# Casting and splitting a weight unit in one piece of 2048 columns instead of two

## The chip, the cores and the metric

The kernel runs on one core of a Trainium2 chip. The core has a matrix engine (TensorE, PE in the profile), a vector engine (VectorE, DVE), a scalar engine (ScalarE, ACT), GpSimd (POOL) and SyncE (SP), which here issues the loads. Each engine works through its own queue in order; semaphores hold an instruction back until what it reads is there. The metric is the time of one execution in microseconds (us), the median of several runs.

## The reference

Two layers over 256 tokens of width 1024, in f32. Each layer projects the normed tokens with one wide matrix, runs two branches (a chunked gated linear attention in both directions, and a grouped-query attention with rotary positions), merges them behind sigmoid gates, and adds an FFN of hidden width 2816 and a gated embedding:

```python
u = rms_norm(h, g_mix_pre)
(gq, gk, gv, gg, ra_f, ra_b, aq, ak, av, gate_a, gate_b) = jnp.split(u @ w_in, offsets, axis=-1)
...
branch_a = (o_gla * jax.nn.silu(gg)) @ w_o_gla
...
branch_b = gqa_attention(q, k, v) @ w_o_attn
mixed = jax.nn.sigmoid(gate_a) * branch_a + jax.nn.sigmoid(gate_b) * branch_b
h = h + rms_norm(mixed @ w_out, g_mix_post)
gate, up = jnp.split(rms_norm(h, g_ffn_pre) @ w_ffn_in, 2, axis=-1)
h = h + rms_norm((jax.nn.silu(gate) * up) @ w_ffn_out, g_ffn_post)
e = p_i @ w_ple_proj
h = h + rms_norm(jax.nn.sigmoid(h @ w_ple_gate) * e, g_ple_post)
```

All weights together are about 160 MB and are read once; the tokens stay on the chip.

## The kernel before

Every matrix product is done as three products of parts in fp32r, a narrower form of f32: each operand x is split into hi = x cast to fp32r and lo = x - hi, and `mm3` (line 96) adds hi x hi, hi x lo and lo x hi in PSUM. So each weight must be cast and split on the chip before TensorE can use it. ACT makes the cast (line 110), DVE the subtraction (line 106), both in `split`.

The weights come in units of 1 MB: 128 partitions by 2048 columns (2112 for the units of the first projection), which is 512 rows of a matrix by 512 of its columns, laid out as four steps of 128 rows, or 256 rows by 1024. The list `plan` holds all 170 units in the order in which they are used. `Stream` carries them:

- `start` issues the loads on SP into raw buffers (pool `rawp`, two of them; in the FFN some units are loaded into borrowed buffers instead, the `lent` and `big` tiles).
- `put` (line 263) takes a pair of buffers wh and wl (pool `wp`, four pairs), puts them on the list `ready`, and gives the cuts in which the unit is to be split: two halves of 1024 columns. The callers `made` and `fill` run `split` on each cut: a cast to wh on ACT and a subtraction to wl on DVE.
- `take` (line 315) hands the oldest unit of `ready` to the matmuls; `done` (line 319) says that a unit is used up, and `fill` then makes the next one, until `held` units (ready or in use) reach `depth`, which is 4, and 3 in the stretch of the linear attention, where a pair of buffers holds that branch's values.

`ready` is a list at the time when the program is written out: it tells how many units stand in program order ahead of the matmuls that are still to come, not how many are finished on the chip at some moment. `open` becomes true after the first units of the start-up, which are ordered by hand.

The order of the instructions in each engine's queue isn't the program's own: a scheduler lays it out when the program is built, by priority (the program's order, moved forward by `tc.high_priority` for norms, transposed activations and some evictions) and by when it expects an instruction's inputs. `tc.issue_after` fixes an order by hand in some places. On the chip each queue runs in the order laid out.

Other parts that the steps below touch: `by_half` takes four units at once and uses them for the first and then the second 128 tokens, as do the first two FFN blocks; `seven` computes two FFN blocks with seven products instead of eight, for which `step` adds raw units on DVE (lines 287 to 298, 2048 columns each) and line 582 combines products; `transpose_in` (line 402) and `turn` transpose activations on TensorE and split them; `pre_norm` and `post_norm_add` compute the norms (squares on ACT line 440, root on POOL, scaling on DVE lines 460 and 500). In names of tiles the number is the layer and the word the stage: rq and kv are the first projections, gqk, v and gg those of the linear attention, then gate, merge, wout, ffnin, ffnout, emb and ple.

Of the kernel before, what the change touches and what calls it, by code (L numbers as in the profile page):

```python
# [48 lines left out]
def trunk_kernel(ctx: ExitStack, tc: tile.TileContext, a: dict, out: bass.AP):  # L49
# [21 lines left out]
    def nm(s):  # L71
        uid[0] += 1
        return f"{s}_{part[0]}_{uid[0]}"
# [134 lines left out]
    class Stream:  # L208
# [51 lines left out]
                    between()  # L260
                x.n = sum(math.prod(dst.shape[1:]) for dst, _ in moves)

        def put(self, x, parts=2):

            wh = wp.tile([P, UNIT], F32R, tag="wh", name=nm("wh"))
            wl = wp.tile([P, UNIT], F32R, tag="wl", name=nm("wl"))
            self.ready.append((wh, wl))
            self.held += 1
            cuts = [slice(j * x.n // parts, (j + 1) * x.n // parts) for j in range(parts)]
            return [(wh[:, c], wl[:, c], x.raw[:, c]) for c in cuts]  # L270

# [1164 lines left out]
```

## Time and profile before

| what | value |
|---|---|
| time, three runs | 934.88, 935.49, 937.68 us; median 935.49 |
| profiled execution, span from first to last instruction | 937.3 us |
| granted TensorE clock over the span | 0.999 |
| PE / weight loads / DVE / ACT busy | 922.6 / 783.9 / 732.4 / 561.6 us |
| casts of units on ACT | 340, two for each of 170 units |
| subtractions of units on DVE | 340 |
| data read from memory | 167.41 MB, 180 GB/s over the span |

The profiled execution's own time is told only as its span, 937.3 us; that is 1.8 us above the median of the runs and within their spread. In the rows of the profile, "x2" is the number of instructions in the row, the two numbers at the head of a timeline row are its start and length in us, and what stands in square brackets is the engine's idle time before the row and what ended it. In rows of groups, busy time and the mean in ns follow the first bar, idle time the second. A matmul's end is modelled, so PE's pace is read from starts.

### The profile page before, as it was taken

The page shows a single profiled execution, that of the slowest core. Times are in us where ns is not written, and L with a number is a line of the kernel's source. Part 1 is how long each engine was busy: PE and PEld are TensorE (multiplying, and loading weights), DVE is VectorE, ACT ScalarE, POOL GpSimd, SP SyncE. Part 2 cuts the span into 40 slices and gives each one's busy share as a digit, 9 for nine tenths or more (in the row PEclk, how much of TensorE's full clock was granted, in tenths as well). Part 3 has the DMA queues.
Part 4 walks back from the last instruction along what each step waited for, and adds up shares of the span by engine and source line. Part 5 has one row for each costly group of instructions (what it writes and reads, how often), then busy time and mean ns, then how long its engine had stood idle before and what let it go on. Part 6 is the DMA issues. An engine that isn't in the chain of part 4 may idle for free.

```text
span 937.3 us, 12331 instructions
## 1 busy us (share of the span) xinstructions
PE 922.6 (98%) x4697; PEld 783.9 (84%) x4697; DVE 732.4 (78%) x933; ACT 561.6 (60%) x928; POOL 80.8 (9%) x150
## 2 busy tenths in 40 slices
PE   8999999999999999999999999999999999999996
PEld 6998888888878878888899988888888788888786
DVE  4798978456569899999689799674666798989874
ACT  4669676443457565567666686754435666656563
POOL 3400214000000000000022001200001000000000
PEclk9999999999999999999999999999999999999999
DMA  6464455665275565547455525365553937463551
GB/s 229 168 223 137 136 191 191 191 213 180 91 249 169 203 233 190 203 143 249 167 175 181 192 78 180 116 244 181 200 190 103 310 114 268 154 266 112 180 180 45
DMA packets 88089, 169.26 MB, mean 181 GB/s; under 512 B 3351, under 2 KB 26391, under 8 KB 88030
## 3 DMA queue, kind: packets, MB, share of 16 engines
q1 hardware_dynamic: 88030, 168.47, 52.8%
q8 instruction: 37, 0.61, 0.3%
q14 instruction: 22, 0.18, 0.1%
HBM read 167.41 MB, written 1.05 MB: 180 GB/s over the span
## 4 chain that ended last, share of the span: by engine, by line
PE 79%; DVE 9%; DMA 4%; ACT 3%; issue 3%; POOL 1%; SPq 0%; POOLq 0%; ACTq 0%; DVEq 0%
PE acc_1ffnin L94 9%; PE acc_0ffnin L94 8%; PE acc_0gate L94 5%; PE acc_1gate L94 5%; PE acc_1merge L94 5%; PE acc_0merge L94 5%; PE acc_0ffnin L543 4%; PE acc_1ffnin L543 4%; PE acc_1gqk L94 2%; PE acc_0rq L94 2%; PE acc_0gqk L94 2%; PE acc_1ple L94 2%; PE acc_0gg L94 2%; PE acc_1gg L94 2%; PE acc_1v L94 2%
## 5 line engine op out<-in xcount | busy, mean ns | idle before, releaser
L94 PE MATMUL acc_1ffnin<-wh_1ffnin,big_1ffnin 128*128 128x512 f32 x176 | 56.9, 393 | 0.0
L94 PE MATMUL acc_0ffnin<-wh_0ffnin,big_0ffnin 128*128 128x512 f32 x176 | 56.8, 392 | 0.0
L110 ACT CAST wh_1ffnin<-raw_1ffnin 128x1024 fp32r<-128x1024 f32 x38 | 38.1, 1050 | 23.1 <-PE acc_1ffnin L94 7.7
L110 ACT CAST wh_0ffnin<-raw_0ffnin 128x1024 fp32r<-128x1024 f32 x38 | 37.9, 1049 | 22.0 <-PE acc_0ffnin L94 7.9
L106 DVE TENSOR_TENSOR wl_1ffnin<-raw_1ffnin,wh_1ffnin 128x1024 fp32r<-128x1024 f32 x38 | 44.8, 1219 | 5.6 <-ACT wh_1ffnin L110 5.4
L106 DVE TENSOR_TENSOR wl_0ffnin<-raw_0ffnin,wh_0ffnin 128x1024 fp32r<-128x1024 f32 x38 | 44.7, 1219 | 3.9 <-ACT wh_0ffnin L110 3.9
L94 PEld LDWEIGHTS acc_1ffnin<-wh_1ffnin,big_1ffnin 128*128 128x128 f32 x176 | 33.0, 188 | 7.1 <-ACT big_1ffnin L110 0.4
L94 PEld LDWEIGHTS acc_0ffnin<-wh_0ffnin,big_0ffnin 128*128 128x128 f32 x176 | 33.0, 188 | 6.7
L106 DVE TENSOR_TENSOR wl_0ffnin<-lent_0ffnin,wh_0ffnin 128x1024 fp32r<-128x1024 f32 x30 | 35.5, 1218 | 1.9 <-ACT wh_0ffnin L110 1.7
L106 DVE TENSOR_TENSOR wl_1ffnin<-lent_1ffnin,wh_1ffnin 128x1024 fp32r<-128x1024 f32 x30 | 35.4, 1218 | 2.0 <-ACT wh_1ffnin L110 2.0
L110 ACT CAST wh_1ffnin<-lent_1ffnin 128x1024 fp32r<-128x1024 f32 x30 | 30.2, 1049 | 9.0 <-PE acc_1ffnin L94 3.0
L110 ACT CAST wh_0ffnin<-lent_0ffnin 128x1024 fp32r<-128x1024 f32 x30 | 30.2, 1049 | 8.4 <-PE acc_0ffnin L94 3.7
L94 PE MATMUL acc_0ffnin<-wl_0ffnin,big_0ffnin 128*128 128x512 f32 x88 | 34.3, 389 | 0.0
L94 PE MATMUL acc_1ffnin<-wl_1ffnin,big_1ffnin 128*128 128x512 f32 x88 | 34.3, 389 | 0.0
L94 PE MATMUL acc_1ffnin<-wh_1ffnin,big_1wout 128*128 128x512 f32 x96 | 31.2, 394 | 0.0
L94 PE MATMUL acc_0ffnin<-wh_0ffnin,big_0wout 128*128 128x512 f32 x96 | 31.2, 394 | 0.0
L543 PE MATMUL acc_0ffnin<-wh_0ffnin,mid_0ffnin 128*128 128x512 f32 x96 | 31.0, 390 | 0.0
L543 PE MATMUL acc_1ffnin<-wh_1ffnin,mid_1ffnin 128*128 128x512 f32 x96 | 31.0, 390 | 0.0
L106 DVE TENSOR_TENSOR wl_0gate<-raw_0gate,wh_0gate 128x1024 fp32r<-128x1024 f32 x14 | 16.5, 1221 | 17.8 <-ACT wh_0gate L110 17.8
L106 DVE TENSOR_TENSOR wl_1gate<-raw_1gate,wh_1gate 128x1024 fp32r<-128x1024 f32 x14 | 16.5, 1221 | 17.8 <-ACT wh_1gate L110 17.8
L94 PE MATMUL acc_0rq<-wh_start,big_start 128*128 128x384 f32 (+1 forms) x96 | 25.4, 349 | 1.4 <-ACT big_start L120 1.4
L94 PE MATMUL acc_0gate<-wh_0gate,big_start 128*128 128x512 f32 x80 | 24.8, 389 | 0.0
(647 smaller groups left out, 2931.3 us busy)
## 6 DMA issues: line engine op xcount, KB each, us to landing
raw_0ffnin<-in_w_ffn_out_dram SPq DMA_DIRECT2D x11, 1024.0 KB, 5.3
raw_1ffnin<-in_w_ffn_out_dram SPq DMA_DIRECT2D x11, 1024.0 KB, 5.9
lent_0ffnin<-in_w_ffn_in_dram SPq DMA_DIRECT2D x6, 1024.0 KB, 8.7
lent_1ffnin<-in_w_ffn_in_dram SPq DMA_DIRECT2D x6, 1024.0 KB, 7.8
raw_0rq<-in_w_in_dram SPq DMA_DIRECT2D x4, 1024.0 KB, 5.2
raw_0v<-in_w_in_dram SPq DMA_DIRECT2D x4, 1024.0 KB, 5.0
raw_0gg<-in_w_in_dram SPq DMA_DIRECT2D x4, 1024.0 KB, 5.1
raw_0gate<-in_w_o_gla_dram SPq DMA_DIRECT2D x4, 1024.0 KB, 5.2
```

The costliest lines, as they stand in the source:

```text
L94: return nc.tensor.matmul(o, lhsT, rhs, start=start, stop=stop)
L106: nc.vector.tensor_tensor(out=out, in0=in0, in1=in1, op=ALU.subtract)
L110: nc.scalar.copy(hi, src)
L543: nc.tensor.matmul(o, x, y, start=first and k + n == 0, stop=k == 3 and n == 2, skip_group_check=not first)
```

## The change

`put` takes its number of pieces from the state of the stream: one piece where the stream is open and the list `ready` holds another unit besides the new one, two where it doesn't. The one piece is one cast of 2048 columns on ACT and one subtraction of 2048 columns on DVE, which waits for the whole cast. Loads, buffers and matmuls are as before.

```diff
-        def put(self, x, parts=2):
+        def put(self, x, parts=None):
 
             wh = wp.tile([P, UNIT], F32R, tag="wh", name=nm("wh"))
             wl = wp.tile([P, UNIT], F32R, tag="wl", name=nm("wl"))
             self.ready.append((wh, wl))
             self.held += 1
+            parts = parts or (1 if self.open and len(self.ready) > 1 else 2)
             cuts = [slice(j * x.n // parts, (j + 1) * x.n // parts) for j in range(parts)]
             return [(wh[:, c], wl[:, c], x.raw[:, c]) for c in cuts]
```

## The prediction, made before the changed kernel was run

> **What bounds the kernel now.** I read the page first: the busy shares, then the chain that ended last.
>
> ```profile
> span 937.3 us, 12331 instructions
> ...
> PE 922.6 (98%) x4697; PEld 783.9 (84%) x4697; DVE 732.4 (78%) x933; ACT 561.6 (60%) x928; POOL 80.8 (9%) x150
> ...
> PE 79%; DVE 9%; DMA 4%; ACT 3%; issue 3%; POOL 1%; SPq 0%; POOLq 0%; ACTq 0%; DVEq 0%
> ```
>
> TensorE (PE) is busy 922.6 of 937.3 us, so it is the bound, and all of its idle time together is 14.7 us. That includes the start, where the first load is waited for, and the tail, where the last norm and the store run after the last matmul. An edit that touches no matmul can win only a part of these 14.7 us. What it can lose has no such limit: each time PE must wait longer for a weight unit, the end moves by that much. The chain says who is last when PE does wait: in 9% of the span VectorE (DVE), in 4% a transfer, in 3% ScalarE (ACT). So next I asked how full DVE is, stage by stage, by windows (columns: PE, PEld, DVE, ACT, POOL busy, granted clock, DMA share, GB/s), here for the FFN stage of each layer.
>
> ```profile
> 283.00:437.00 154.00, 153.32 (x697) 126.25 (x696) 144.90 (x141) 95.81 (x120) 1.82 (x3) 1.00 0.56 195
> ...
> 742.00:896.00 154.00, 152.36 (x690) 124.85 (x690) 142.65 (x138) 94.28 (x118) 0.86 (x2) 1.00 0.55 194
> ```
>
> In the FFN, DVE is busy 144.90 of 154 us, 94%, and PE still only idles 0.7 us. DVE is nearly a second bound there, but the queue of finished units hides it. The clock granted is 1.00 in both, so it plays no part.
>
> **The price of one piece.** The groups by line and shape, and one stretch of the chain that gives PE's pace:
>
> ```profile
> L110 ACT CAST wh_0gate<-raw_0gate 128x1024 fp32r<-128x1024 f32 x14 | 14.0, 1052 | 14.0 <-PE acc_0gate L94 13.9
> ...
> L106 DVE TENSOR_TENSOR wl_0gate<-raw_0gate,wh_0gate 128x1024 fp32r<-128x1024 f32 x14 | 16.5, 1221 | 17.8 <-ACT wh_0gate L110 17.8
> ...
> L287 DVE TENSOR_TENSOR lent_0ffnin<-lent_0ffnin,lent_0ffnin 128x2048 f32<-128x2048 f32 x3 | 6.9, 2285 | 0.0
> ...
> 418.63 5.44 PE acc_0ffnin L543 x24
> ```
>
> A cast of 1024 columns takes 1.05 us, a subtraction 1.22 us. A DVE tensor_tensor of 2048 columns in f32 exists already (line 287): 2.285 us. Two halves back to back take 2.35 or 2.36 us (rows below), so one piece saves 0.07 us of DVE. For the cast no 2048 row exists. It lies between 1.85 us (if only 0.80 us were added to 1.05) and 2.00 us, which is what two halves take back to back in the rows below. I take 1.90 us, because merging on DVE saved a little less than 0.1 us too. PE's pace is 5.44/24 = 0.23 us a matmul.
>
> [...]
>
> How many units: each layer's plan has 4 rank units, 22 of the projection, 8 merge, 4 w_out, 42 FFN, 1 embedding and 4 gate units, 85, so 170. Three are made before the stream is open, and five with nothing else ready (the first unit after w_out, after the four units that the FFN takes at once, and after the first layer's last gate stage). The other 162 become one piece: 162 casts and 162 subtractions fewer, about 16 us less ACT and 11 us less DVE. In the gate rows the casts' idle time is ended by PE (13.9 of 14.0): there a unit is made as soon as a buffer comes free, three units ahead of its use. In these stages I cost the edit at nothing, and the lead of several us is the cover. No DMA is added or moved on SP's queue. A raw buffer comes free 0.07 us earlier where the halves ran back to back, and about 0.8 us later where DVE had stood waiting for the cast.
>
> That is the catch. With halves, DVE starts 1.05 us after the cast does, and after about 2.3 us PE can use the first half (two of the unit's four contraction steps). With one piece, hi is there after 1.90 us and lo after 1.90 + 0.04 + 2.285 = 4.23 us, 1.9 us later for the first use. Being "ready" is counted when the program is written out, not by time: a unit whose load lands late is number three or four of the list and is just as late. So I looked for each place where PE takes a unit within 2 us of its completion, or waits for a DVE result queued behind one.
>
> **B and C, FFN entry, layers 0 and 1** (timelines of ACT, DVE and PE):
>
> ```profile
> 264.10 2.00 ACT L110 CAST wh_0wout<-raw_0wout 128x1024 fp32r<-128x1024 f32 x2 [1.94 <-DMA raw_0wout<-in_w_ffn_in_dram]
> 265.19 2.36 DVE L106 TENSOR_TENSOR wl_0wout<-raw_0wout,wh_0wout 128x1024 fp32r<-128x1024 f32 x2 [0.48 <-ACT wh_0wout L110]
> 266.47 0.50 PE L94 MATMUL acc_0ffnin<-wl_0wout,big_0wout 128*128 128x512 f32 x1 [0.23 <-DVE wl_0wout L106]
> 269.36 1.38 PE L402 MATMUL aux_0wout<-ident,mid_0wout 128*128 128x128 f32 x8
> 269.89 2.35 DVE L106 TENSOR_TENSOR wl_0wout<-raw_0wout,wh_0wout 128x1024 fp32r<-128x1024 f32 x2
> 271.16 0.50 PE L94 MATMUL acc_0ffnin<-wl_0wout,big_0wout 128*128 128x512 f32 x1 [0.18 <-DVE wl_0wout L106]
> ...
> 721.98 2.01 ACT L110 CAST wh_1wout<-raw_1wout 128x1024 fp32r<-128x1024 f32 x2 [1.06 <-DMA raw_1wout<-in_w_ffn_in_dram]
> 723.39 2.35 DVE L106 TENSOR_TENSOR wl_1wout<-raw_1wout,wh_1wout 128x1024 fp32r<-128x1024 f32 x2
> 724.84 0.39 PE L94 MATMUL acc_1ffnin<-wl_1wout,big_1wout 128*128 128x512 f32 x1
> 727.92 2.35 DVE L106 TENSOR_TENSOR wl_1wout<-raw_1wout,wh_1wout 128x1024 fp32r<-128x1024 f32 x2
> 729.19 0.50 PE L94 MATMUL acc_1ffnin<-wl_1wout,big_1wout 128*128 128x512 f32 x1 [0.18 <-DVE wl_1wout L106]
> ```
>
> The cast waits for its transfer, and PE waits for the first half. In one piece: cast 264.10 to 266.00, subtraction 266.04 to 268.33, first lo use 268.37 instead of 266.47, 1.90 us late. PE then has eleven matmuls (2.50), eight transposes (0.87 at the 0.11 us they take start to start) and one matmul (0.23), 3.60 us, and would reach the next unit's lo at 271.97. It is there at 269.89 + 2.285 + 0.04 = 272.21 instead of 271.16. The short waits that PE has in between now vanish in this, so the net loss is 1.05 us. Layer 1 the same way: cast to 723.88, lo at 726.24 instead of 724.84 (1.40 late); the next unit is reached at 729.84 and ready at 730.24 against 729.19: 1.05 us.
>
> **A, first keys unit of layer 0.** DVE is full of rotary work:
>
> ```profile
> 45.01 1.21 DVE L106 TENSOR_TENSOR wl_0rq<-raw_start,wh_0rq 128x1024 fp32r<-128x1024 f32 x1
> ...
> 46.28 0.50 PE L94 MATMUL acc_0kv<-wl_0rq,big_start 128*128 128x512 f32 x1 [0.15 <-DVE wl_0rq L106]
> ...
> 46.61 1.21 DVE L106 TENSOR_TENSOR wl_0rq<-raw_start,wh_0rq 128x1024 fp32r<-128x1024 f32 x1
> ```
>
> One piece from 45.01 ends at 47.30, so PE goes on at 47.35 instead of 46.28: 1.07 us.
>
> **D, end of the FFN, layer 0 and layer 1, and F, the second pair's start:**
>
> ```profile
> 427.78 2.00 ACT L110 CAST wh_0ffnin<-raw_0ffnin 128x1024 fp32r<-128x1024 f32 x2 [0.75 <-DMA raw_0ffnin<-in_w_ffn_out_dram]
> 429.11 2.35 DVE L106 TENSOR_TENSOR wl_0ffnin<-raw_0ffnin,wh_0ffnin 128x1024 fp32r<-128x1024 f32 x2
> 430.50 0.40 PE L94 MATMUL acc_0ffnin<-wl_0ffnin,big_0ffnin 128*128 128x512 f32 x1
> ...
> 877.30 2.00 ACT L110 CAST wh_1ffnin<-raw_1ffnin 128x1024 fp32r<-128x1024 f32 x2 [4.51 <-DMA raw_1ffnin<-in_w_ffn_out_dram]
> 878.39 2.36 DVE L106 TENSOR_TENSOR wl_1ffnin<-raw_1ffnin,wh_1ffnin 128x1024 fp32r<-128x1024 f32 x2 [1.73 <-ACT wh_1ffnin L110]
> 884.14 0.68 DVE L103 TENSOR_TENSOR t_1ffnin<-mid_1ffnin,t_1ffnin 128x512 f32<-128x512 f32 x1
> 884.88 0.66 PE L402 MATMUL aux_1ffnin<-ident,t_1ffnin 128*128 128x128 f32 x4 [1.48 <-DVE t_1ffnin L103]
> 886.46 2.00 ACT L110 CAST wh_1ffnin<-raw_1ffnin 128x1024 fp32r<-128x1024 f32 x2
> 890.15 0.40 PE L94 MATMUL acc_1ffnin<-wl_1ffnin,big_1ffnin 128*128 128x512 f32 x1
> ...
> 327.00 2.00 ACT L110 CAST wh_0ffnin<-raw_0ffnin 128x1024 fp32r<-128x1024 f32 x2 [1.21 <-DMA raw_0ffnin<-in_w_ffn_in_dram]
> 330.36 0.68 DVE L582 TENSOR_TENSOR mid_0ffnin<-acc_0ffnin,mid_0ffnin 128x512 f32<-128x512 f32 x1
> 331.19 0.47 PE L543 MATMUL acc_0ffnin<-wh_0ffnin,big_0wout 128*128 128x512 f32 x1 [0.55 <-DVE mid_0ffnin L582]
> ```
>
> Layer 0 at 430: cast to 429.68, lo at 432.04 against 430.50: 1.54 us. Layer 1: DVE starts the unit at 879.24 instead of 878.39 and is done 0.78 us later; one more unit in between gives 0.07 back, so the product that PE's transposes await moves from 884.14 to 884.86, 0.72 us. The cast at 886.46, behind these transposes, moves to 887.18, lo is there at 891.44 against 890.15: 1.29 us in all. F: cast to 328.90, DVE to 331.23; the combination behind it (line 582), which frees PE's accumulator, starts at 331.15 instead of 330.36: 0.79 us.
>
> **E, hand-over to layer 1.** PE waits for a unit's second half, then for the norm:
>
> ```profile
> 481.97 0.41 PE L94 MATMUL acc_1rq<-wl_0ple,big_0ple 128*128 128x288 f32 x1 [0.39 <-DVE wl_0ple L106]
> ...
> 483.57 0.66 PE L402 MATMUL aux_0ple<-ident,mid_0ple 128*128 128x128 f32 x4 [0.53 <-DVE mid_0ple L460]
> ```
>
> The unit would come later, but PE waits for the norm at 483.57 anyway. A whole unit on DVE ahead of the norm's steps can hold it about 1.2 us (half a unit), and a raw buffer freed sooner can start the last load 1.2 us sooner. Between -1.2 and +1.2 I take 0.
>
> **Sum.** 1.07 + 1.05 + 1.05 + 1.54 + 1.29 + 0.79 = 6.79 us. For the shorter DVE queue I take off 0.4 us: in each FFN one wait behind three merged units, 3 x 0.07 twice. Net +6.4 us on a span of 937.3. The profiled span lies 1.8 us above the median of the runs, 935.49, so the forecast is 935.5 + 6.4 = 941.9 us. If no wait in between is absorbed (B 1.90, C 1.40, E 1.2) the loss is about 10 us. If the order of DVE's work is written out anew so that half of the places vanish, it is 3 us. I cannot see that order: the engines' queues are laid out by priority and expected readiness, and fewer, longer instructions can change it.
>
> **Rivals.** (1) Faster. DVE is at 94% in the FFN; its relief there is 38 units x 0.07 = 2.7 us a layer, and the waits at 331.19 and 884.88 (0.55 and 1.48 us) end on DVE. If the queue ahead of such a wait holds several merged units and no late cast, PE gets it all: about 3.2 us from both, with the short waits, 932.3 us. It decides if the unit ahead is not held by its transfer. Against it: at both places DVE's queue begins with a late load. [...] (2) No change: the late first halves are absorbed by other waits or taken out by a new order. What remains is 0 to 2.5 us, about 936.5 us. For it: at B a loss of 1.90 shrinks to 1.05 within 5 us, and E to nothing. (3) Worse: each late unit also frees its raw buffer 0.8 us late, and with two such buffers the next-but-one load is late too. Where loads set the casts (all FFN ends), three or four links add 5 us: 947 us or more. Against it, most units have leads of over 2 us.
>
> **Chances.** Forecast 0.52, rival 1 0.15, rival 2 0.25, rival 3 0.08. About 0.3%, 2.8 us, is what a measurement can tell from no change. Slower by more than that: 0.60, same 0.25, faster 0.15. The range of the forecast alone is 938.5 to 946 us; with the rivals down to a tenth below and a little above, 933 to 947 us.
>
> **What would show it.** The casts and subtractions of units: 178 of each instead of 340, at 1.90 and 2.29 us. PE's idle time up by some 6 us, as waits on a lo tile at the FFN entry (lo use 1.9 us after now) and near 430 and 890, and on line 582 near 331. DVE's busy time about 721 us, ACT's about 546. PE's matmul busy time per stage unchanged. I am wrong if the FFN entry shows no longer wait, if PE's idle time falls below 14 us, or if the cast of 2048 columns takes well under 1.85 us.

## The result, and the profile after

The changed kernel takes 960.48 us (median of four runs, 955.97 to 961.37); the kernel before took 936.22 us beside it. The ratio is 1.0236, 95% interval 1.0218 to 1.0254: 24 us slower, where the prediction said 6.4. The profiled execution has a span of 958.5 us, 21.2 more than before. First the page, with the groups of the new pieces in the FFN:

```profile
span 958.5 us, 12013 instructions
...
PE 930.7 (97%) x4697; PEld 787.6 (82%) x4697; DVE 722.1 (75%) x771; ACT 547.6 (57%) x766; POOL 89.3 (9%) x150
...
PE 74%; DVE 9%; DMA 7%; ACT 4%; issue 3%; POOL 2%; SPq 0%; POOLq 0%; ACTq 0%; DVEq 0%
...
L110 ACT CAST wh_0ffnin<-raw_0ffnin 128x2048 fp32r<-128x2048 f32 x19 | 36.1, 1913 | 32.5 <-PE acc_0ffnin L94 10.2
...
L106 DVE TENSOR_TENSOR wl_0ffnin<-raw_0ffnin,wh_0ffnin 128x2048 fp32r<-128x2048 f32 x19 | 43.3, 2290 | 12.2 <-ACT wh_0ffnin L110 12.1
```

The pieces cost what they should: 1.91 us a cast, 2.29 a subtraction. 162 instructions fewer stand on each of the two engines, DVE is busy 10.3 us less and ACT 14.0 less. All of it came off engines whose total is not the bound, and PE stands idle 27.8 us instead of 14.7. PE's waits, longest first (total us, times, longest):

```profile
PE aux_1ffnin L1259 <- DVE t_1ffnin L103: 3.9, 1, 3.9
PE acc_0ffnin L94 <- DVE wl_0wout L106: 2.4, 2, 1.8
PE aux_0ffnin L1259 <- DVE t_0ffnin L103: 2.0, 1, 2.0
PE acc_0kv L94 <- DVE wl_0rq L106: 2.0, 1, 2.0
PE aux_0ple L403 <- DVE mid_0ple L461: 1.9, 2, 1.2
PE acc_1ffnin L94 <- DVE wl_1wout L106: 1.6, 2, 1.1
...
PE aux_1at L94 <- DVE big_1kv L106: 1.3, 1, 1.3
PE aux_1at L94 <- ACT big_1kv L110: 0.8, 1, 0.8
PE aux_1at L94 <- DVE mid_1at L106: 0.7, 1, 0.7
```

Rows on wl are waits for a unit: A (wl_0rq), B (wl_0wout) and C (wl_1wout) of the prediction. Rows on t, mid and big are waits for activations, which only stand in the same queues as the units. They are as large, and the prediction has none of them but E (mid_0ple). I call them G (349 us, t_0ffnin), I (819 us, t_1ffnin) and H (531 us, the transposed keys). The third part is PE's clock (windows; the granted clock is the third column from the right):

```profile
48.00:54.00 6.00, 6.00 (x21) 4.74 (x20) 4.69 (x8) 1.75 (x6) 1.04 (x3) 0.72 0.91 312
271.00:275.00 4.00, 3.84 (x20) 3.01 (x20) 3.28 (x3) 3.45 (x5) 0.60 (x2) 1.00 0.73 218
...
353.00:357.00 4.00, 4.00 (x14) 3.18 (x14) 2.07 (x3) 0.79 (x3) 0.00 (x0) 0.61 0.53 127
...
533.64:537.05 3.41, 2.89 (x13) 2.89 (x14) 1.51 (x4) 0.00 (x0) 0.00 (x0) 0.50 0.90 291
...
819.60:823.60 4.00, 0.12 (x1) 0.00 (x0) 4.00 (x5) 1.90 (x1) 0.00 (x0) 1.00 0.01 5
823.60:827.20 3.60, 3.58 (x11) 2.80 (x12) 3.19 (x3) 0.59 (x1) 0.00 (x0) 0.53 0.02 3
```

Behind A, G and I the granted clock of these windows is 0.72, 0.61 and 0.53, and the 512-column matmuls there start 0.43 us apart instead of 0.23. Behind H the window is laid on the slow stretch itself: 0.50 for 3.41 us. The other three slow stretches are as long. Behind the shorter wait B (1.8 us) the clock is 1.00 in the window from 271 us. Worked out from PE's starts over the whole trace, gaps of over 0.25 us beyond the usual distance add some 15 us, and matmuls at a slow pace some 6. Together that is the 21.2 us of the span.

### The profile page after: what moved, and what is told of

It is laid out like the page before. It is cut to its first block, busy times and chain, and to the rows that moved or that the text cites. A ratio compares the mean times of both kernels' runs of the same rounds, so it can differ in the third digit from the quotient of the medians.

```text
span 958.5 us, 12013 instructions
## 1 busy us (share of the span) xinstructions
PE 930.7 (97%) x4697; PEld 787.6 (82%) x4697; DVE 722.1 (75%) x771; ACT 547.6 (57%) x766; POOL 89.3 (9%) x150
## 3 DMA queue, kind: packets, MB, share of 16 engines
HBM read 167.41 MB, written 1.05 MB: 176 GB/s over the span
## 4 chain that ended last, share of the span: by engine, by line
PE 74%; DVE 9%; DMA 7%; ACT 4%; issue 3%; POOL 2%; SPq 0%; POOLq 0%; ACTq 0%; DVEq 0%
PE acc_1ffnin L94 9%; PE acc_0ffnin L94 8%; PE acc_0ffnin L544 5%; PE acc_1ffnin L544 5%; PE acc_0gate L94 5%; PE acc_1gate L94 5%; PE acc_1merge L94 5%; PE acc_0merge L94 5%; PE acc_0rq L94 2%; PE acc_0gqk L94 2%; PE acc_1ple L94 2%; PE acc_0gg L94 2%; PE acc_1gg L94 2%; PE acc_0v L94 2%; PE acc_1gqk L94 1%
## 5 line engine op out<-in xcount | busy, mean ns | idle before, releaser
L110 ACT CAST wh_0ffnin<-raw_0ffnin 128x2048 fp32r<-128x2048 f32 x19 | 36.1, 1913 | 32.5 <-PE acc_0ffnin L94 10.2
L110 ACT CAST wh_1ffnin<-raw_1ffnin 128x2048 fp32r<-128x2048 f32 x19 | 36.1, 1912 | 28.7 <-PE acc_1ffnin L94 10.3
L106 DVE TENSOR_TENSOR wl_0ffnin<-raw_0ffnin,wh_0ffnin 128x2048 fp32r<-128x2048 f32 x19 | 43.3, 2290 | 12.2 <-ACT wh_0ffnin L110 12.1
L106 DVE TENSOR_TENSOR wl_1ffnin<-raw_1ffnin,wh_1ffnin 128x2048 fp32r<-128x2048 f32 x19 | 43.3, 2290 | 11.1 <-ACT wh_1ffnin L110 11.0
L106 DVE TENSOR_TENSOR wl_1ffnin<-lent_1ffnin,wh_1ffnin 128x2048 fp32r<-128x2048 f32 x15 | 34.3, 2287 | 6.2 <-ACT wh_1ffnin L110 6.2
L106 DVE TENSOR_TENSOR wl_0ffnin<-lent_0ffnin,wh_0ffnin 128x2048 fp32r<-128x2048 f32 x15 | 34.3, 2288 | 5.5 <-ACT wh_0ffnin L110 5.4
L110 ACT CAST wh_1ffnin<-lent_1ffnin 128x2048 fp32r<-128x2048 f32 x15 | 28.7, 1914 | 11.2 <-PE acc_1ffnin L94 3.0
L110 ACT CAST wh_0ffnin<-lent_0ffnin 128x2048 fp32r<-128x2048 f32 x15 | 28.7, 1916 | 10.7 <-PE acc_0ffnin L544 3.6
L94 PE MATMUL acc_1ffnin<-wh_1ffnin,big_1wout 128*128 128x512 f32 x96 | 31.2, 394 | 0.0
L106 DVE TENSOR_TENSOR wl_0gate<-raw_0gate,wh_0gate 128x2048 fp32r<-128x2048 f32 x7 | 16.1, 2293 | 19.1 <-ACT wh_0gate L110 19.1
L544 PE MATMUL acc_1ffnin<-wh_1ffnin,big_1wout 128*128 128x512 f32 x72 | 24.9, 409 | 0.0
```

The source lines that it names most:

```text
L94: return nc.tensor.matmul(o, lhsT, rhs, start=start, stop=stop)
L106: nc.vector.tensor_tensor(out=out, in0=in0, in1=in1, op=ALU.subtract)
L110: nc.scalar.copy(hi, src)
L544: nc.tensor.matmul(o, x, y, start=first and k + n == 0, stop=k == 3 and n == 2, skip_group_check=not first)
```

## The experiments

My first reading was that the queues had been laid out anew: in the kernel before, the silu products at I stand between units, in the changed one behind them. To hold the order fixed, most kernels here write each engine's whole queue out by hand:

```diff
         trunk_kernel(tc, aps, out)
+        in_order(tc, nc, ORDER)   # ORDER: the positions of each engine's instructions
...
+        for p, i in zip(seq, seq[1:]):
+            tc.add_manual_dep(i, p.name, <order only, no wait>)
```

**Length against order (e1 to e4).** e1: whole pieces, the order of the kernel before. e2: halves, the new order. e3: as e1, at the second half's place. e4: the new order, but 33 instructions round G and I in the old one.

> The changed kernel's whole units, but every engine's queue written out in the order that it has in the kernel before, each whole cast and subtraction in the place of its unit's first half. Two theories. Order: most of the 24 us comes from the queues being laid out anew, so this run keeps only the late first halves of the prediction (A, B and C, 1.1 to 2.1 us each) and a few short operations that stand behind a whole piece: 938 to 943 us. Piece: the length itself costs the time, since a whole unit of 1.9 us on ScalarE and 2.29 us on VectorE holds up what stands behind it, in whatever order: 953 to 960 us.

> The reverse: the kernel before's two halves, but every engine's queue in the order of the changed kernel, the second half right behind the first. Order: the waits of the changed kernel stay (G 2.2, I 4.1, H 2.5, the hand-over 1.9 us more, the clock's slow stretches behind them), only the late first halves at A, B and C go: 952 to 956 us. Piece: about the time of the kernel before, 936 to 940 us.

> As e1, but each whole cast and subtraction in the place of its unit's second half, so that what stood between the two halves in the kernel before is no longer behind it. Order: the waits behind a whole piece go, the first halves are later still where TensorE is close behind: 936 to 942 us, and the difference to e1 tells which of the two costs more. Piece: 953 to 960 us.

> The changed kernel with its own order, but for 33 instructions of ScalarE and VectorE in two places (the FFN at about 349 us and at about 819 us), which stand in the order of the kernel before: the silus, their products and the pair's products ahead of the unit instead of behind it. Order: the two waits G 2.15 and I 4.06 us go, and with them the matmuls at half pace behind them (about 1.5 us each): 950 to 953 us. Piece: the work stands behind whole units anyhow, 958 to 961 us.

| kernel | us | ratio to before (95%) |
|---|---|---|
| e1 whole, old order | 964.43 | 1.0277 (1.0235 to 1.0318) |
| e2 halves, new order | 941.70 | 1.0041 (1.0026 to 1.0056) |
| e3 whole, old order, later place | 961.89 | 1.0256 (1.0220 to 1.0291) |
| e4 whole, 33 instructions in old order | 961.19 | 1.0247 (1.0219 to 1.0275) |

The theory of order fell: no run came into its ranges. All four lie 0.2 to 4.4 us above the ranges that I gave the piece. The order by itself costs 3.9 us, the length 27 us in the old order (22 to 30 by the interval), and which half's place the piece takes makes no difference beyond the intervals. Writing the queues out costs nothing by itself: e16 below, which has the kernel before written out with other pieces for five units alone, takes 0.9994 of its time. In e4 the wait at I is nearly as long as ever, and at G it is longer than in the changed kernel (3.9 us by PE's starts instead of 2.15):

```profile
821.42 0.27 PE L1259 MATMUL aux_1ffnin<-ident,t_1ffnin 128*128 128x128 f32 x1
825.88 0.60 PE L1259 MATMUL aux_1ffnin<-ident,t_1ffnin 128*128 128x128 f32 x3 [3.72 <-DVE t_1ffnin L103]
```

**Where, and which of the two instructions (e5 to e8).** Four kernels in the old order: whole only outside the FFN (82 units), only in the FFN (80), only the cast whole, only the subtraction whole. The edits are in `put` and `split`:

```diff
-parts = parts or (1 if self.open and len(self.ready) > 1 else 2)
+parts = parts or (1 if self.open and len(self.ready) > 1 and x.make not in ffn else 2)   # e5; "in ffn" in e6
+for c in casts: nc.scalar.copy(hi[:, c], src[:, c])                                      # e7: one cut of casts, two of subs
+for c in subs: vsub(lo[:, c], src[:, c], hi[:, c].bitcast(F32))                          # e8: two and one
```

> Queues in the order of the kernel before, as in e1, but only the 82 units outside the FFN whole, the 80 of the FFN in halves. Theory Idle: the first half being longer lets each subtraction begin 0.9 us later, VectorE, whose queue is in order, stands idle for that (in e1 134.7 us behind casts of units instead of 93.9), and where it is near its bound, in the FFN at 93% busy, TensorE pays for it. Outside the FFN only the waits that e1 has there stay (A, B, C, about 137 to 147 and 565 to 620 us, together about 9 us): 943 to 948 us. Rival, that the cost lies in all stages alike: about half of e1's 27 us, 950 to 952 us.

> The complement of e5: only the 80 units of the FFN whole, the others in halves, the order of the kernel before. Theory Idle: e1's waits at 327 to 442 and at 798 to 915 us stay, 11 us over the kernel before, and half-pace stretches behind the longest: 950 to 954 us; e5 and e6 together add up to about e1's 27 us. If the FFN's units had slack: 938 to 942 us.

> The order of the kernel before, ScalarE's cast whole, VectorE's subtraction in two halves. From the start of a cast the first low half stands after 1.9 + 1.17 = 3.1 us (halves 2.2, whole 4.2), the unit after 4.25 us (halves 3.35, whole 4.2). Theory Idle: VectorE waits as long as in e1, so most of the cost stays, 957 to 964 us. Rival First half (the prediction's): TensorE waits for the first low half alone, so about half of the cost goes: 948 to 952 us.

> The reverse: ScalarE's cast in two halves, VectorE's subtraction whole, in the place of the first. First low half and unit both after 2.0 + 2.29 = 4.3 us. Theory Idle and theory First half: as e1, 960 to 966 us. Rival, that a long cast on ScalarE holds up the silus and splits of activations behind it: the cost goes with the long cast, 938 to 948 us.

Beside 937.60 us for the kernel before: e5 945.59 (1.0085, 1.0060 to 1.0110), e6 955.63 (1.0196, 1.0167 to 1.0225), e7 955.97 (1.0206, 1.0174 to 1.0239), e8 979.14 (1.0443, 1.0417 to 1.0469). 8.0 and 18.0 us add up to 26, e1's 27 within its interval; e6 is 1.6 us above its range. A long cast on ScalarE isn't needed for the loss: e8 has none and is the slowest, 13 us above the range that I gave both theories. I put that down to its one subtraction, which stands in the first half's place and waits for the second cast, further back in ScalarE's queue, and so holds up VectorE. That makes e8 no clean test: how much of the loss comes from a long cast holding up other work on ScalarE stays open. e7 came out between the two ranges that I gave it: the long cast alone costs 18 us, and the late first low half is part of the rest. At A PE waits 0.60 us in e7 and 2.08 in e1; there it is mostly the length of the subtraction.

**Load, or one unit's own way (e9, e10), and the other direction (e12).** e9 and e10 drop the four additions in `step` with whole units and with halves. e12 has `4 if ... else 2` pieces.

> As e1 (whole units, the order of the kernel before), with the 24 sums of 128x2048 left out that the pairs of the FFN need on VectorE (2.28 us each, 55 us in all; so the FFN's outputs are not the reference's). Theory Idle, VectorE near its bound: with a third of a VectorE stage's other work gone, the FFN's waits under whole units go, and only what e5 keeps outside the FFN stays: 941 to 948 us. Rival Latency, that TensorE waits because a unit's own way from free buffer to low half is 0.9 to 2 us longer, however busy VectorE is: 955 to 962 us.

> The control of e9: units in halves, the order of the kernel before, the same 24 sums left out. TensorE waits only 7 us in the kernel before, so both theories expect little: 932 to 938 us.

> The other direction: the 162 units in four pieces of 512 columns, the order of the kernel before, two quarters in the place of each half. Theory Idle: a subtraction can begin 0.45 us sooner still, VectorE's idle time behind casts falls under 93.9 us, but its busy time grows by about 162 x 2 x 0.06 = 19 us: the two nearly cancel, 933 to 941 us. Theory Latency: every unit is ready earlier, 931 to 936 us. Rival, that instructions' fixed costs decide on a busy VectorE: 945 us and over.

Beside 937.98 us: e9 954.12 (1.0176, 1.0155 to 1.0196), e10 935.26 (0.9973, 0.9962 to 0.9983), e12 938.00 (1.0006, 0.9996 to 1.0016). Without the sums whole units cost 18.9 us in all instead of 27, so 8 us go with VectorE's load (mostly through the clock, as the last table of this section shows). e9 misses the range that I gave the load theory (Idle) by 6 us and that of Latency by 1. Quarters change nothing, as Idle expected and Latency did not: VectorE idles 72.7 us behind casts of units instead of 93.9 (134.7 in e1, all summed from the traces), and is busy about as much longer.

**The clock (e11, e13).** Needless transposes into the tile that the waiting ones overwrite:

```diff
                         ps = aux()
+                        for _ in range(FILL[l] if b == PLAIN[2] else 0):   # FILL = (16, 32); e11: PLAIN[1]
+                            nc.tensor.transpose(ps[:, :P], ident, ident)
```

> The changed kernel in its own order, with 16 and 32 needless transposes of the identity on TensorE in the two waits G and I (349 and 819 us), written into the tile that the waiting transposes overwrite; 0.11 us each, so they end before the wait does. Theory Clock: the half pace behind these waits comes from TensorE standing still for over 2 us; with the filling the granted clock stays at 1.00 and the 512-column matmuls behind at 0.23 us: 3 us less, 956 to 958 us. Rival, that the pace has another cause in the same place: the slow matmuls stay at 0.43 us and the time at 960 us.

> As e11, but the 16 and 32 needless transposes stand directly ahead of the transposes that wait at G and I (the block after the one of e11). Theory Clock: TensorE no longer stands still for over 2 us there, the granted clock stays at 1.00 in the 4 us behind (0.61 and 0.53 in the changed kernel), the 512-column matmuls there come every 0.23 us, 3 us less in all: 956 to 959 us. Rival: slow matmuls and time as in the changed kernel.

e11 took 956.48 us (1.0206, 1.0174 to 1.0237). I had put both fillings, 5 us of work, one block too early, the second at 798 us. So it is luck that the time lies in the range of Clock: the slow stretches behind G and I are still there (granted clock 0.61 from 823.4 to 827.4 us). The kernel was no slower than the changed one for the 5 us: the wait I shrank from 4.1 to 2.0 us. That fits queues of units and activations that set the time there, and not PE. e13 took 953.96 us (1.0172, 1.0145 to 1.0199), 2 us under the range of Clock. Its windows over the filling at I, and the 4 us behind it:

```profile
815.90:819.60 3.70, 3.66 (x33) 3.42 (x31) 3.70 (x4) 1.91 (x1) 0.00 (x0) 1.00 0.03 10
819.60:823.60 4.00, 3.81 (x21) 3.20 (x22) 3.92 (x5) 1.18 (x2) 0.00 (x0) 1.00 0.10 14
```

The clock stays at 1.00 where it was 0.53, and 21 matmuls fit into 4.0 us instead of 11 into 3.6. So the slow stretch at I comes from PE standing still, as far as one profiled execution can show it. In the four runs of e13 the granted clock over the span was 0.996 to 0.999, in those of the changed kernel 0.989 to 0.994. Of the gain over the changed kernel, 2.0 us lie in this FFN. The rest lies where no filling stands (2.9 us near H, whose slow stretch did not occur in this execution, and 1.6 at the hand-over), so the whole run's time does not price the clock. At G a wait of 2.4 us stayed behind the filling, here with no slow stretch after it.

**Which units pay (e14 to e16).** `len(self.ready) > 3` (60 units), `1 < len(self.ready) < 4` (102), and four pieces only where `len(self.ready) == 1`.

> Whole only the 60 units that are put when three others stand ready (48 of them in the gates, the merge and the first stages, 12 in the FFN), the order of the kernel before. Theory Late: a whole unit costs only where TensorE comes to it soon, so these cost almost nothing but for the keys' unit at A (1.8 us): 938 to 941 us. Rival, all units alike, since each keeps VectorE idle for a longer cast: 60 of 162 of e1's 27 us, 948 us.

> The other 102 units whole, those put with one or two others ready (66 of them in the FFN). Theory Late: nearly all of e1's 27 us, less the keys' unit: 959 to 963 us. All alike: 102 of 162, 955 us.

> The kernel before, but the five units behind which no other stands ready in four pieces instead of two: TensorE's waits for a first low half (0.40 and 0.43 us at the FFN's entry of layer 0, 0.43 in layer 1, 0.5 at the hand-over) get about 0.3 us shorter each, no other unit changes: 936 to 938 us, at best 1.5 us under the kernel before.

Beside 937.80 us: e14 948.38 (1.0109, 1.0083 to 1.0135), e15 953.31 (1.0164, 1.0130 to 1.0197), e16 937.22 (0.9994, 0.9978 to 1.0010). Both e14 and e15 miss the ranges of Late, by 7 and 6 us: by the medians the cost follows the number of units, as the rival "all alike" said. The traces show otherwise. The table gives how much later than in the kernel before PE starts the first matmul of a stage, from the profiled executions (at the start they differ by up to 1.6 us, from the first load):

| first matmul of | before, us | after | e1 | e5 | e9 | e14 | e17 | e18 |
|---|---|---|---|---|---|---|---|---|
| 0gqk | 45.05 | -0.70 | -0.66 | -0.26 | -0.46 | -1.62 | -1.57 | -1.43 |
| 0v | 79.18 | +2.91 | +1.11 | +1.55 | +1.35 | +1.78 | +1.85 | -1.43 |
| 0merge | 192.08 | +2.87 | +2.76 | +3.38 | +3.07 | +1.79 | +3.27 | -1.43 |
| 0ffnin | 260.38 | +2.87 | +2.76 | +3.38 | +3.08 | +1.79 | +3.27 | -1.43 |
| 0ple | 447.52 | +8.14 | +13.56 | +4.13 | +8.48 | +7.73 | +7.98 | -3.05 |
| 1rq | 472.19 | +10.67 | +13.56 | +4.14 | +8.48 | +7.73 | +8.00 | -3.04 |
| 1gate | 603.28 | +15.30 | +16.15 | +6.79 | +10.92 | +8.09 | +8.81 | -3.19 |
| 1ffnin | 719.14 | +15.25 | +17.01 | +7.63 | +11.77 | +8.09 | +9.66 | -3.19 |
| 1ple | 906.98 | +21.17 | +25.65 | +8.49 | +15.18 | +11.16 | +13.54 | -4.44 |

In e14 the gates and merges, 32 of its 60 units, cost nothing (+1.79 from 0v to 0ffnin, +8.09 from 1gate to 1ffnin). What it loses, it loses at A, with the w_out unit that is used at the FFN's entry, and with a dozen units in the FFN. From 0merge to 0ffnin no version loses anything. So `ready`, counted in program order, does not tell a unit's slack; the stage does.

**The ring of raw buffers (e17, e18).** The two raw buffers are used in turn, as a ring. F in e1 is where one unit's 0.79 us became 1.4. SP's issues (SPq), ACT, DVE and PE of e1:

```profile
325.80 4.49 DVE L106 TENSOR_TENSOR wl_0ffnin<-raw_0ffnin,wh_0ffnin 128x2048 fp32r<-128x2048 f32 x2 [2.03 <-ACT wh_0ffnin L110]
328.12 0.92 SPq L257 DMA_DIRECT2D raw_0ffnin<-in_w_ffn_in_dram  x2
333.84 1.91 ACT L110 CAST wh_0ffnin<-raw_0ffnin 128x2048 fp32r<-128x2048 f32 x1 [1.82 <-DMA raw_0ffnin<-in_w_ffn_in_dram]
335.78 2.29 DVE L106 TENSOR_TENSOR wl_0ffnin<-raw_0ffnin,wh_0ffnin 128x2048 fp32r<-128x2048 f32 x1 [1.75 <-ACT wh_0ffnin L110]
337.99 0.68 DVE L583 TENSOR_TENSOR mid_0ffnin<-acc_0ffnin,mid_0ffnin 128x512 f32<-128x512 f32 x1
338.82 0.47 PE L544 MATMUL acc_0ffnin<-wh_0ffnin,big_0wout 128*128 128x512 f32 x1 [1.96 <-DVE mid_0ffnin L583]
```

and the kernel before:

```profile
318.73 4.63 DVE L106 TENSOR_TENSOR wl_0ffnin<-raw_0ffnin,wh_0ffnin 128x1024 fp32r<-128x1024 f32 x4 [1.29 <-ACT wh_0ffnin L110]
321.11 0.92 SPq L257 DMA_DIRECT2D raw_0ffnin<-in_w_ffn_in_dram  x2
```

From the cast to the combination it is 4.15 us instead of 3.36: the predicted 0.79. But the load too was issued later: 7.01 us after the same load of the kernel before, while PE, at the start of its wait, was only 6.2 us behind (336.47 against 330.25). It had waited for its raw buffer, which the subtraction of an earlier whole unit had freed late: the first of the two that begin at 325.80 us ends 2.29 us later, at 328.09, and the load is issued at 328.12.

```diff
-rawp = ctx.enter_context(tc.tile_pool(name="rawp", bufs=2))
+rawp = ctx.enter_context(tc.tile_pool(name="rawp", bufs=3))
-b4p = ctx.enter_context(tc.tile_pool(name="b4p", bufs=10))
+b4p = ctx.enter_context(tc.tile_pool(name="b4p", bufs=8))
```

> As e1 (whole units, the order of the kernel before), with three raw buffers for the loads instead of two, and eight instead of ten 1024-column tiles to make room. Theory Ring: with two buffers a load waits until the unit two ahead is split, so each late unit makes a later one late again; a third buffer lets the load start a unit sooner. The FFN's waits shrink to those of the one late unit, and the half-pace stretches behind them go: 942 to 950 us. Rival, VectorE's queue alone: the unit is split 0.8 to 2 us later whenever its load lands, 958 to 964 us.

> The control of e17: the kernel before with three raw buffers and eight 1024-column tiles. TensorE waits 7 us in all in the kernel before, some of it behind units whose load was late: 932 to 938 us; above 940 us the two tiles fewer would cost something by themselves.

Beside 938.32 us: e17 952.47 (1.0159, 1.0142 to 1.0177), e18 934.46 (0.9960, 0.9947 to 0.9973). The same place in e17:

```profile
330.29 1.92 ACT L110 CAST wh_0ffnin<-raw_0ffnin 128x2048 fp32r<-128x2048 f32 x1 [0.57 <-DVE wl_0ffnin L106]
332.24 2.29 DVE L106 TENSOR_TENSOR wl_0ffnin<-raw_0ffnin,wh_0ffnin 128x2048 fp32r<-128x2048 f32 x1 [0.78 <-ACT wh_0ffnin L110]
334.44 0.68 DVE L583 TENSOR_TENSOR mid_0ffnin<-acc_0ffnin,mid_0ffnin 128x512 f32<-128x512 f32 x1
```

The cast no longer waits for a transfer, and PE's wait there falls from 2.1 to 0.9 us. With three buffers whole units cost 18.0 us instead of 27: the ring is about a third of it, and e17 misses the range that I gave the ring by 2.5 us. e18 is the fastest version found, 0.4% under the kernel before; its gain lies in the FFNs (1.6 and 1.3 us by the table).

The next table adds up PE's waits of over 0.15 us after the start-up by what they were for, and counts the slow stretches of 3.41 us at a granted clock of 0.50 before PE's last matmul, in which at most 1.7 us each are lost:

| profiled execution | before | after | e1 | e2 | e9 | e10 | e17 | e18 |
|---|---|---|---|---|---|---|---|---|
| waits for a unit (wh, wl), us | 1.1 | 7.0 | 13.4 | 1.6 | 9.7 | 1.0 | 8.7 | 0.6 |
| for an activation or a sum of products, us | 3.0 | 10.6 | 8.1 | 7.1 | 8.0 | 0.8 | 5.9 | 1.5 |
| slow stretches | 0 | 4 | 3 | 1 | 0 | 0 | 1 | 0 |

PE waits 17.4 us longer in e1 than in the kernel before, 15.9 longer in e9 than in e10, and 12.5 longer in e17 than in e18. So the load takes only 1.5 us off the waits; most of its 8 us is that e9's execution has none of e1's three slow stretches. The ring takes 4.9 us off the waits, and two slow stretches.

What stays open: load and ring take about 8 and 9 us off, but were not tried together, so they may be partly the same 8 us. The remaining 10 or more I put down to the longer way of each unit and the activations behind it; no run takes these apart.

## Why the prediction was wrong, step by step

- **Price of one piece.** Right: 1.90 and 2.285 us forecast, 1.91 and 2.29 measured; 178 of each. The lower bound of the cast supposed 0.80 us for the second 1024 columns; they took 0.86 us (1.91 less 1.05).
- **B and C.** The mechanism was right, the size 0.3 us short at each. The rows of the changed kernel:

```profile
266.64 1.91 ACT L110 CAST wh_0wout<-raw_0wout 128x2048 fp32r<-128x2048 f32 x1 [1.69 <-DMA raw_0wout<-in_w_ffn_in_dram]
268.58 2.29 DVE L106 TENSOR_TENSOR wl_0wout<-raw_0wout,wh_0wout 128x2048 fp32r<-128x2048 f32 x1 [1.08 <-ACT wh_0wout L110]
270.93 0.49 PE L94 MATMUL acc_0ffnin<-wl_0wout,big_0wout 128*128 128x512 f32 x1 [1.83 <-DVE wl_0wout L106]
275.39 0.50 PE L94 MATMUL acc_0ffnin<-wl_0wout,big_0wout 128*128 128x512 f32 x1 [0.55 <-DVE wl_0wout L106]
...
745.76 0.50 PE L94 MATMUL acc_1ffnin<-wl_1wout,big_1wout 128*128 128x512 f32 x1 [0.52 <-DVE wl_1wout L106]
```

The first low half is used 4.29 us after its cast began, before 2.37: 1.92 us later, 1.90 forecast. At the second unit PE goes on at 275.39 instead of 271.16 us, in layer 1 at 745.76 instead of 729.19. Less the delay with which it entered the stage (2.87 and 15.25 us) that is a loss of 1.36 and 1.32 us, 1.05 forecast.
- **A.** The unit came when forecast, but the loss was larger:

```profile
45.16 2.28 DVE L106 TENSOR_TENSOR wl_0rq<-raw_start,wh_0rq 128x2048 fp32r<-128x2048 f32 x1
...
47.50 0.50 PE L94 MATMUL acc_0kv<-wl_0rq,big_start 128*128 128x512 f32 x1 [1.98 <-DVE wl_0rq L106]
```

PE goes on at 47.50 us, 47.35 forecast. But PE was 0.7 us earlier than before, waited for that too, and then ran 3.4 us at half pace: +3.6 us from 0gqk to 0v, 1.07 forecast; 1.8 in e1, where no slow stretch followed.
- **D and F.** Wrong for the changed kernel, about right in the old order. PE waits neither near 430 nor for the combination of line 582 (583 in the changed kernel) near 331, and the wait of 1.6 us at 884 is gone. PE arrives later there, which I take for the reason. In e1 D's wait in layer 0 is 1.87 us (1.54 forecast) and F's is 2.1, 1.4 more than before (0.79 forecast), since the ring doubles it. The same wait in layer 1, which the prediction does not list, is 2.6 us in e1 (810 us).
- **E.** 2.5 us from 0ple to 1rq, outside the bounds of 1.2. It needs the new order: e1 has 0.0 there. But halves in that order (e2) lose only 0.9, and e13, with whole units, 1.0, so some 1.5 of the 2.5 stay unexplained.
- **"In these stages I cost the edit at nothing ... the lead of several us is the cover", and the list of places behind it.** This is the step that failed. For the gates and merges of the changed kernel it is right. But the list holds only places where PE waits, or nearly waits, in the trace of the kernel before; all others were put at nothing, and a new order was only expected to take places away. An activation's silu, product or split has no such lead. PE's waits for units did grow by 5.9 us, near the sum of 6.4, but that is luck: D and F are not there, and A, B and C are larger. The waits for activations grew by 7.6 us (G, I, H and the wait at 568 us come to 2.15 + 4.06 + 2.48 + 0.83 = 9.5 us, and an older one is gone), and none of these four was in the sum. VectorE's rows at I in the kernel before, where PE doesn't wait:

```profile
797.26 0.42 DVE L103 TENSOR_TENSOR t_1ffnin<-acc_1ffnin,t_1ffnin 128x256 f32<-128x256 f32 x1
...
799.79 2.35 DVE L106 TENSOR_TENSOR wl_1ffnin<-big_1ffnin,wh_1ffnin 128x1024 fp32r<-128x1024 f32 x2
...
802.92 2.28 DVE L290 TENSOR_TENSOR lent_1ffnin<-lent_1ffnin,big_1ffnin 128x2048 f32<-128x2048 f32 x1
805.12 0.42 DVE L103 TENSOR_TENSOR t_1ffnin<-acc_1ffnin,t_1ffnin 128x256 f32<-128x256 f32 x1
```

in the changed kernel:

```profile
818.15 2.28 DVE L106 TENSOR_TENSOR wl_1ffnin<-big_1ffnin,wh_1ffnin 128x2048 fp32r<-128x2048 f32 x1
820.35 2.28 DVE L291 TENSOR_TENSOR lent_1ffnin<-lent_1ffnin,big_1ffnin 128x2048 f32<-128x2048 f32 x1
...
823.16 0.74 DVE L103 TENSOR_TENSOR t_1ffnin<-acc_1ffnin,t_1ffnin 128x256 f32<-128x256 f32 x2
823.62 0.39 PE L1259 MATMUL aux_1ffnin<-ident,t_1ffnin 128*128 128x128 f32 x1 [3.90 <-DVE t_1ffnin L103]
```

and in e2, with halves in the same order:

```profile
801.33 2.35 DVE L106 TENSOR_TENSOR wl_1ffnin<-big_1ffnin,wh_1ffnin 128x1024 fp32r<-128x1024 f32 x2
803.60 2.29 DVE L290 TENSOR_TENSOR lent_1ffnin<-lent_1ffnin,big_1ffnin 128x2048 f32<-128x2048 f32 x1
...
806.40 0.75 DVE L103 TENSOR_TENSOR t_1ffnin<-acc_1ffnin,t_1ffnin 128x256 f32<-128x256 f32 x2
806.87 0.33 PE L1258 MATMUL aux_1ffnin<-ident,t_1ffnin 128*128 128x128 f32 x1 [2.38 <-DVE t_1ffnin L103]
```

In the kernel before the first product that PE awaits stands ahead of the unit; the new order puts it behind a unit and a sum. So e2 already waits 1.3 us at G and 2.55 at I, and whole units make it 2.15 and 4.06. In the old order (e1) G and I are not there, but the waits for units grow by 12 us, 7.4 of which lie in the FFN behind its entry: there the lead doesn't cover PE's own use of a unit either.
- **"It plays no part"** (the clock). Wrong by some 6 us, four slow stretches; in the kernel before, where PE hardly waits, there is none before its last matmul.
- **Rival 3**, 947 us or more, the ring, had 8 in 100. Its mechanism was there (about a third of the cost of e1, by e17), and at F it acts, as the rival said, where a load sets the cast. That "most units have leads of over 2 us" was the wrong argument against it, as the lead is counted to PE and not to the raw buffer.
- **Rival 1**, a shorter VectorE queue. VectorE was relieved of 10 us and PE waited more. (The FFN has 40 whole units a layer, 80 in e6, and not the 38 of the rival; that is 2.8 us instead of 2.7.) Its argument was VectorE's 94% in the FFN. Yet whole units in the FFN alone (e6) cost 18.0 us. Pieces smaller than halves gained nothing either: with quarters (e12) the kernel took 938.00 us beside 937.98.

## What to carry to other kernels

Here a longer piece was also paid by what stood behind it in the queue: at I, in the same order, PE waited 4.06 us with whole units and 2.55 with halves, and at F in e1 a load was issued at 328.12 us, when a whole subtraction had ended at 328.09. So before merging two instructions list not only the consumer of their result but all short work in the same queue that another engine waits for, and the buffer that their end frees. That the total work of a nearly full engine shrinks says nothing of this: VectorE, 94% busy in the FFN, was relieved of 10.3 us, and the kernel took 24 us more. With 51 us of VectorE's work in the FFNs gone (e9) most of the loss was still there, so it is not only a matter of load. If the queues are laid out anew, look at what stands in front of each short instruction in the new order. PE's single waits of 1.43 to 1.95 us ahead of 512-column matmuls cost only themselves in these runs (21 of 21); behind those of 1.97 us and more its pace halved in 27 of 40, and that cost some 1.5 us on top.

## What the runs showed of the hardware

I had not expected that TensorE runs slower behind waits as short as 2.0 us (A). Taking all waits ahead of 512-column matmuls, or of the transposes right before them, in the runs above, by the gap beyond the usual distance of starts: behind none of 21 waits of 1.43 to 1.95 us did the pace halve, behind 17 of 29 of 1.97 to 2.19 us, and behind 10 of 11 of 2.27 us and more. H, ahead of 256-column matmuls, is not among them: there two waits of 1.0 and 1.5 us with 0.6 us of matmuls between them were enough (0.6 and 1.5 us in e4). The half pace lasted 3.41 us at a granted clock of 0.50 in each of the changed kernel's four slow stretches, and cost some 1.5 us (6 us in the four). Why waits of 1.97 to 2.19 us went either way, no run shows.
